# Layer 0 of a two-layer streaming encoder: forgetting attention interleaved with the band attention's projections

## The chip, the cores and the metric

The kernel runs on one core of a Trainium2 chip. The metric is the device time of one execution in microseconds (us), the median of several runs. The engines are named as in the profile: PE (TensorE matmul), PEld (its weight load), DVE (VectorE), ACT (ScalarE), POOL (GpSimd) and SP (SyncE, which issues nearly every DMA here).

## The reference

Two layers of an encoder run over one prompt of 1024 tokens and 8 sample streams of 16 tokens with caches of 512 positions. The change lies in layer 0, cut here to what matters:

```python
def even_proj(h, w_in, b_forget):
    p = h @ w_in                                  # 1152 x 1024 times 1024 x 3080
    qa, ka, va, qb, kb, vb, fa = jnp.split(p, [...], axis=-1)
    logf = jax.nn.log_sigmoid(fa + b_forget)
    ...
# forgetting attention "a": 8 heads of 64, causal, scores + cumsum(logf)[q] - cumsum(logf)[k]
# band attention "b": 8 heads of 64, each chunk of 64 sees itself and 8 chunks to the left, plus a relative bias
y = concat([oa, ob]) @ w_out_even
# sample streams: the 16 new queries of each stream against 512 cached and 16 new keys, in a and in b
```

Then follow a gated feed-forward block, layer 1 with sliding-window attention, another feed-forward block and a final norm.

## The kernel before, in words

Activations lie transposed, channels on the 128 partitions and 1152 tokens along the free dimension. A product at near-float32 precision takes three fp32r matmuls: high part times high part, high times low, low times high (`passes`, lines 166 to 168).

**Projections.** `in_proj` runs "units". A unit 0 to 3 is 128 columns of queries (`proj_q`, line 309), 4 to 7 are 128 columns of keys (`proj_k`, line 344), 8 and 9 are 256 columns of values (`proj_v`, line 361). A q or k unit runs over four chunks of 288 tokens with 24 matmuls each (`chunk_steps`, line 288), a v unit over nine tiles of 128 tokens with 24 matmuls each. Every chunk accumulates in one PSUM bank. `finish` then empties the bank: for keys two ACT copies and a DVE subtraction (lines 348 to 353), for queries an ACT and a DVE instruction (314, 315). The results go to scratch in DRAM by DMA. The bank of a chunk comes from `ps_any`, which goes round the tags m, s, t, s, seven of the eight banks (line 75: s has 3, t 2, m 2, and o has 1).

**Attention.** `prompt_steps` (line 563) yields a head of three steps and then 64 units, each a list of steps: 8 heads of a (the forgetting attention, "fox" below) with four pairs of query tiles, then 8 heads of b. A score step (461) writes 128 queries times up to 1024 keys in banks s and takes the softmax on DVE and ACT. A transpose step (485) turns two key blocks of probabilities and splits them on ACT and DVE, with zeros set by POOL where a block is masked (line 502). A value step (516) multiplies by the values. `attn_load` (427) loads one head.

**Samples.** `sample_steps` (605) handles the 16 pairs of kind and stream. Each loads a cached key tile `skt` and a value tile `svt`. For kind a it also loads a bias tile `sbi`, from which POOL subtracts `cqs` (line 628). A POOL copy spreads the queries into `qbd`.

**Order.** The program states the steps in a written order. `merge` interleaves lists by their weights in proportion. A scheduler of the tile framework then reorders the instructions of each engine by its own model before the program is built. On the chip each engine runs its list strictly in order, and so does SP with its DMA issues. In the kernel before, all units of b's projection are run, then the attention of a and b, with the samples merged along both:

```python
    with sb("pinb", "right") as pin:
        in_proj(1, pin, (0, 1, 8, 2, 3, 9, 4, 5, 6))
        run(pr[0])
        in_proj(1, pin, [7])
    ...
        run(merge(flat(pr[2:]), [(3500, lambda: None)] + sample_steps(pa, qbd, nbs), ...))
```

After layer 0's attention follow the output projection and the feed-forward block (`block_tail`).

Of the kernel before, what the change touches and what calls it, by code (L numbers as in the profile page):

```python
# [11 lines left out]
F32 = mybir.dt.float32  # L12
# [7 lines left out]
P = 128  # L20
D = 1024
KT = D // P
NP = 1024
# [37 lines left out]
def model(ctx: ExitStack, tc: tile.TileContext, I, O):  # L61
# [6 lines left out]
    def sb(name, side="left"):  # L68
        return tc.tile_pool(name=name, bufs=1, side=side, reuse_waits="tile")
# [53 lines left out]
    def nm(s):  # L123
        uid[0] += 1
        return f"{s}_{uid[0]}"
# [32 lines left out]
    def weights(src, shape, other=None, eng=G):  # L158
        f = lambda t: t.rearrange("p (a b) -> p a b", b=shape[1])
        return tuple(f(t) for t in parts(raw_weights(src), other, eng))  # L160
# [123 lines left out]
    def ps_any(tags="msts"):  # L284
        rot[0] += 1
        return ps(tags[rot[0] % len(tags)])
# [19 lines left out]
        return [[((c[3] - c[2]) * 10 // pieces, lambda ci=ci, g=g: part(ci, g)) for g in range(pieces)]  # L306
                for ci, c in enumerate(act)]

    def proj_q(src, act, pool, dst_heads, dst_sample, w=None):
        def finish(o, c0, c1):  # L310
            w = min(c1, NP) - c0
            qh_ = pool.tile([P, c1 - c0], F32R, name=nm("qh"), tag="sth", bufs=2)
            ql_ = pool.tile([P, c1 - c0], F32R, name=nm("ql"), tag="stl", bufs=2)
            A.activation(qh_[:, :w], o[:, :w], AF.Copy, scale=-SCALE)
            V.scalar_tensor_tensor(ql_[:, :w], o[:, :w], -SCALE, qh_[:, :w], ALU.mult, ALU.subtract)
            for r in range(2):
                S.dma_start(dst_heads[r][0:HD, c0:c0 + w], f32(qh_)[r * HD:(r + 1) * HD, :w])
                S.dma_start(dst_heads[r][HD:P, c0:c0 + w], f32(ql_)[r * HD:(r + 1) * HD, :w])
            if c1 > NP:
                qf = pool.tile([P, NS], F32, name=nm("qf"), tag="qf", bufs=1)  # L320
                A.activation(qf, o[:, w:w + NS], AF.Copy, scale=-SCALE)
                S.dma_start(dst_sample, qf)

        return chunk_steps(src, act, ps_any, finish, 1, w)

    def proj_qc(j, act, pool, tiles):

# [13 lines left out]

        return [s_ for l in chunk_steps(I["w_qc"][j], act, lambda: ps("m"), finish, 4) for s_ in l]

    def proj_k(src, act, pool, out, dst_hi, dst_lo, dst_sample, get=ps_any):
        def finish(o, c0, c1):
            w = min(c1, NP) - c0
            kf = pool.tile([P, c1 - c0], F32, name=nm("kf"), tag="kf", bufs=2)
            A.copy(kf, o[:, :c1 - c0])
            S.dma_start(out[:, c0:c1], kf)
            kh_ = pool.tile([P, c1 - c0], F32R, name=nm("khs"), tag="sth", bufs=2)  # L350
            kl_ = pool.tile([P, c1 - c0], F32R, name=nm("kls"), tag="stl", bufs=2)
            A.copy(kh_[:, :w], o[:, :w])
            V.tensor_tensor(kl_[:, :w], o[:, :w], kh_[:, :w], ALU.subtract)
            S.dma_start(dst_hi[:, c0:c0 + w], f32(kh_)[:, :w])
            S.dma_start(dst_lo[:, c0:c0 + w], f32(kl_)[:, :w])
            if c1 > NP:
                S.dma_start(dst_sample, kf[:, w:w + NS])

        return chunk_steps(src, act, get, finish, 1)

    def proj_v(srcs, width, act, pool, nh, dst_out, dst, dst_sample, gate=None):
        per = 4 if len(srcs) == 2 else 8
        ws = [weights(s, (per, width)) for s in srcs]
        wts = [(w[0][:, k, :], w[1][:, k, :]) for w in ws for k in range(per)]
        nv = nh * HD
        for tt in range(T // P):
            t0 = tt * P
            o = ps_any()
            xh_, xl_ = (z[:, :, t0:t0 + P] for z in whole)
            for k in range(KT):  # L370
                E.matmul(o[:, :width], xh_[:, k], wts[k][0], start=k == 0, stop=False)  # L371
                E.matmul(o[:, :width], xh_[:, k], wts[k][1], start=False, stop=False)  # L372
                E.matmul(o[:, :width], xl_[:, k], wts[k][0], start=False, stop=k == KT - 1)  # L373
            vf = pool.tile([P, 256], F32, name=nm("vf"), tag="vf", bufs=2)
            A.copy(vf[:, :nv], o[:, :nv])
            S.dma_start(dst_out[t0:t0 + P], vf[:, :nv])
            if gate is not None:
                V.tensor_tensor(gate[:, tt * 8:(tt + 1) * 8], o[:, 256:264], bfg, ALU.add)
            if tt < NP // P:
                S.dma_start(dst(tt), vf[:, :nv])  # L380
            else:
                S.dma_start(dst_sample, vf[:, :nv])

    def proj_vt(src, act, pool, out, dst_hl, dst_sample):

# [70 lines left out]
        G.tensor_tensor(v[:, :, HD:], vp, v[:, :, :HD], ALU.subtract)  # L456
        return q, kh_, q2, kl2, v, bias

    tiles = [0]

    def score_step(pool, kind, h, tq, un):

        q, kh_, q2, kl2, v, bt = un["hd"]["ins"]
        kb0 = 0 if kind == "a" else max(0, tq - 4)
        n = (tq + 1 - kb0) * P
        tiles[0] += 1
        t = (wp.tile([P, 4 * VW], F32, name=nm("t"), tag="wr", bufs=3) if tiles[0] > 4 and tiles[0] % 3 and (kind == "a" or h < 7 or tq < 4) else
             pool.tile([P, NP], F32, name=nm("t"), tag="t", bufs=4))[:, :NP]
        mins = pool.tile([P, 4], F32, name=nm("mins"), tag="mins", bufs=8)
        segs = []  # L470
        qt = slice(tq * P, (tq + 1) * P)
        for c0, c1 in split(n):
            sp = ps("s")
            w = c1 - c0
            k0 = kb0 * P + c0
            E.matmul(sp[:, :w], q[:, qt], kh_[:, k0:k0 + w], start=True, stop=False)  # L476
            dg = kind == "a" and c1 == n
            E.matmul(sp[:, :w], q2[:, qt], kl2[:, k0:k0 + w], start=False, stop=not dg)  # L478
            if dg:
                E.matmul(sp[:, w - P:w], identb, maskb, start=False, stop=True)  # L480
            segs.append((sp[:, :w], c0, c1, bt[:, 640 - n + c0:640 - n + c1] if bt is not None else
                         zero.to_broadcast([P, w])))
        un[tq] = kb0, t, softmax(pool, t, segs, n, mins)
# [75 lines left out]
    def run(steps):  # L559
        for _, f in steps:  # L560
            f()
# [827 lines left out]
    pq = ExitStack()  # L1389
    pin = pq.enter_context(sb("pina", "right"))  # L1390

    def unit(ki, p, pool, w=None):

        kind = "ab"[ki]
        if p < 4:
            return proj_q(I["w_q"][ki * 4 + p], act, pool, [qs[kind][2 * p], qs[kind][2 * p + 1]],
                          qsm[kind][:, p, :], w)
        p -= 4
        return proj_k(I["w_k"][ki * 4 + p], act, pool, O[f"{kind}_kt"][p * P:(p + 1) * P],
                      kh[kind][p * P:(p + 1) * P], kl[kind][p * P:(p + 1) * P], ksm[kind][:, p, :])  # L1400

    flat = lambda ls: [s_ for l in ls for s_ in l]

    def in_proj(ki, pool, units):
        kind = "ab"[ki]
        for p in units:
            if p < 8:
                run(flat(unit(ki, p, pool)))
                continue
            u = p - 8  # L1410
            first = kind == "a" and u == 0
            src = [I["w_vg"][j] if first else I["w_v"][ki * 2 + u, j] for j in range(2)]
            proj_v(src, VW if first else 256, act, pool, 4, O[f"{kind}_v"][:, u * 256:(u + 1) * 256],
                   lambda tt: vs[kind][:, tt, u * 2:(u + 1) * 2, :],
                   vsm[kind][:, u * 256:(u + 1) * 256], gate if first else None)

    gate = pin.tile([P, 72], F32, name="gate")
    with sb("px0", "right") as px:
# [30 lines left out]
            run(merge(*([flat(f[ci - 1] for f in first)] if ci else []), post[ci], *pre[ci + 1:ci + 2]))  # L1449
        run(flat(f[-1] for f in first))  # L1450
    act = coarse
    in_proj(0, pin, (8, 3, 4, 5, 9))
    forget(nc, pin, nm, ps, gate, ident, ones, I, O, cpd, lsd, csd, cqs)
    in_proj(0, pin, (6, 7))
    pq.close()
    pat = ExitStack()
    pa = pat.enter_context(sb("patin", "right"))
    late = {}
    pr = prompt_steps(pa, late)
    with sb("pinb", "right") as pin:  # L1460
        in_proj(1, pin, (0, 1, 8, 2, 3, 9, 4, 5, 6))
        run(pr[0])
        in_proj(1, pin, [7])
    in0.close()

    xst = ExitStack()
# [2 lines left out]
        xp[h] = xst.enter_context(sb(f"x{h}"))  # L1469
    X = [[None] * 4 for _ in range(2)]  # L1470
    pages, pgs = [], []
    late["p"] = pat.enter_context(sb("patout", "right"))
    with sb("samp", "right") as pa:
        nbs = pa.tile([P, SK], F32, name="nbs")
        S.dma_start(nbs, I["bias_bs"])
        G.tensor_scalar(nbs, nbs, -1.0, 1.0, ALU.mult, ALU.mult)
        qbd = [pa.tile([P, 4, 32], F32, name=f"qbd{i}") for i in range(2)]
        for z in qbd:
            G.memset(z, 0.0)
        run(pr[1])  # L1480
        def behind(f):
            with tc.issue_after(marks["q"].ins):
                f()

        ld = x_load(lambda h, i: I["x"][:, 2 * i:2 * i + 2, h * HALF:(h + 1) * HALF])
        run(merge(flat(pr[2:]), [(3500, lambda: None)] + sample_steps(pa, qbd, nbs), [(4, lambda: None)] + [(1, lambda f=f: behind(f)) for _, f in ld]))
    pat.close()


# [200 lines left out]
```

## Time and profile before

| | us |
|---|---|
| median of 3 runs | 2833.36 (2829.34 to 2841.15) |
| the profiled execution, own time | 2836.8 |
| span of its core, first to last instruction | 2834.7 |
| mean granted TensorE clock, share of 2.4 GHz | 0.977 |
| PE busy | 2712.7 (96%) |
| DVE / ACT / POOL busy | 1697.9 (60%) / 1167.3 (41%) / 1312.6 (46%) |
| projections of b without attention beside them | about 160 to 338 |
| attention of a and b with the samples | about 338 to 700 |

Times of places are counted from the span's start. A PE that is busy all the time is not a PE at its peak, since matmuls are pipelined and their ends are modelled. So the starts of matmuls, their number per us and the weight loads (PEld) are read beside it.

### The profile page before, as it was taken

The numbers are of one execution on the slowest core, as the hardware profiler recorded it, in microseconds if no ns is written. First come the engines' busy times: TensorE is split into PE (matmuls) and PEld (weight loads), VectorE is DVE, ScalarE is ACT, GpSimd is POOL, SyncE is SP. The second block draws the span as 40 slices with busy tenths as digits, with TensorE's granted clock in tenths as the row PEclk, the third lists the DMA queues.
The fourth block names the chain that finished last, engine by engine and source line by source line (L and its number), as shares of the span: only waits on it lengthen the run. The fifth ranks groups of instructions, "written<-read, shape, count | busy, mean of one in ns | idle before, by whom it ended". The sixth has DMA issues, their size and how long they took to land.

```text
span 2834.7 us, 53673 instructions
## 1 busy us (share of the span) xinstructions
PE 2712.7 (96%) x20254; PEld 2563.1 (90%) x20254; DVE 1697.9 (60%) x3676; ACT 1167.3 (41%) x2510; POOL 1312.6 (46%) x1418
## 2 busy tenths in 40 slices
PE   8999999999989999999998999989899999999987
PEld 7999967776989999999998988978799999999987
DVE  7110266666585555656677756663956555566677
ACT  5221367666443222223332467674432222223323
POOL 4212133333444444444998443242444444448993
PEclk8999999999999999999999999999999999999998
DMA  5546579773322222326432232142222232255422
GB/s 158 172 138 199 183 209 261 219 223 106 112 78 72 98 97 95 104 79 232 149 115 80 72 104 62 37 139 62 77 72 100 81 98 100 95 194 182 115 65 93
DMA packets 205971, 349.17 MB, mean 123 GB/s; under 512 B 25992, under 2 KB 136720, under 8 KB 203664
## 3 DMA queue, kind: packets, MB, share of 16 engines
q1 hardware_dynamic: 201104, 341.03, 38.5%
q10 hardware_dynamic: 4608, 4.72, 0.5%
q8 instruction: 159, 2.61, 0.4%
q14 instruction: 100, 0.82, 0.1%
HBM read 243.84 MB, written 101.82 MB: 122 GB/s over the span
## 4 chain that ended last, share of the span: by engine, by line
PE 76%; DVE 9%; POOL 5%; issue 5%; DMA 4%; ACT 2%; SPq 0%; DVEq 0%; POOLq 0%; ACTq 0%
PE ps L166 19%; PE ps L167 19%; PE ps L168 19%; PE ps L499 2%; POOL pg L260 2%; PE ps L478 2%; PE ps L524 1%; PE ps L476 1%; PE ps L372 1%; PE ps L373 1%; PE ps L371 1%; DVE hf L256 1%; PE ps L531 1%; DMA oraw<-od 1%; PE ps L752 1%
## 5 line engine op out<-in xcount | busy, mean ns | idle before, releaser
L166 PE MATMUL ps<-pg,wh 128*128 128x288 f32 x3200 | 951.1, 299 | 42.9 <-DVE x L1257 27.1
L167 PE MATMUL ps<-pg,wh 128*128 128x288 f32 x3200 | 952.2, 298 | 4.0 <-POOL pg L260 2.7
L168 PE MATMUL ps<-pg,wh 128*128 128x288 f32 x3200 | 935.8, 295 | 0.2 <-DVE wh L260 0.2
L166 PEld LDWEIGHTS ps<-pg,wh 128*128 128x128 f32 x3200 | 606.0, 190 | 48.7 <-DVE x L1257 27.6
L167 PEld LDWEIGHTS ps<-pg,wh 128*128 128x128 f32 x3200 | 608.1, 190 | 6.7 <-POOL pg L260 3.5
L168 PEld LDWEIGHTS ps<-pg,wh 128*128 128x128 f32 x3200 | 603.7, 190 | 1.8 <-issue 1.0
L260 POOL TENSOR_TENSOR wh<-wr,wh 128x1024 fp32r<-128x1024 f32 (+1 forms) x96 | 232.9, 2429 | 344.5 <-ACT wh L259 334.5
L259 ACT CAST wh<-wr 128x1024 fp32r<-128x1024 f32 (+2 forms) x156 | 161.3, 1037 | 244.0 <-PE ps L168 218.8
L167 PE MATMUL ps<-hl,wh 128*128 128x288 f32 x832 | 247.4, 299 | 2.5 <-DVE hl L260 2.3
L166 PE MATMUL ps<-hh,wh 128*128 128x288 f32 x832 | 245.7, 301 | 3.4 <-ACT hh L259 3.1
L168 PE MATMUL ps<-hh,wh 128*128 128x288 f32 x832 | 244.9, 296 | 0.0
L260 POOL TENSOR_TENSOR pg<-pg,pg 128x576 fp32r<-128x576 f32 x126 | 193.6, 1551 | 25.6 <-ACT pg L259 24.2
L1257 DVE TENSOR_TENSOR x<-x,ps 128x288 f32<-128x288 f32 x384 | 156.3, 447 | 77.0 <-PE ps L168 76.5
L259 ACT CAST pg<-pg 128x576 fp32r<-128x576 f32 (+1 forms) x134 | 90.6, 701 | 271.2 <-PE ps L168 147.2
L260 POOL TENSOR_TENSOR wh<-x,wh 128x1024 fp32r<-128x1024 f32 x42 | 101.3, 2411 | 150.1 <-ACT wh L259 150.1
L167 PEld LDWEIGHTS ps<-hl,wh 128*128 128x128 f32 x832 | 158.0, 190 | 4.4 <-DVE hl L260 3.4
L166 PEld LDWEIGHTS ps<-hh,wh 128*128 128x128 f32 x832 | 156.5, 190 | 5.5 <-ACT hh L259 5.0
L260 POOL TENSOR_TENSOR x<-wr,x 128x512 fp32r<-128x512 f32 x44 | 58.6, 1331 | 216.5 <-ACT x L259 216.5
L168 PEld LDWEIGHTS ps<-hh,wh 128*128 128x128 f32 x832 | 157.9, 190 | 0.1
L1117 DVE TENSOR_TENSOR u<-p,ps 128x288 f32<-128x288 f32 x176 | 79.0, 449 | 113.3 <-PE ps L168 112.9
L507 DVE TENSOR_TENSOR pl<-ps,ph 128x512 fp32r<-128x512 f32 (+1 forms) x152 | 92.7, 615 | 38.7 <-ACT ph L506 34.2
L166 PE MATMUL ps<-x,wh 128*128 128x288 f32 x352 | 105.7, 300 | 3.8 <-DVE x L1121 3.8
(297 smaller groups left out, 6420.0 us busy)
## 6 DMA issues: line engine op xcount, KB each, us to landing
wr<-w_ffn_in SPq DMA_DIRECT2D x88, 512.0 KB
hds<-hd SPq DMA_DIRECT2D x252, 144.0 KB
pg<-hds SPq DMA_DIRECT2D x126, 288.0 KB
wd<-w_ffn_out SPq DMA_DIRECT2D x36, 512.0 KB
wr<-w_out SPq DMA_DIRECT2D x22, 512.0 KB
xd<-x SPq DMA_DIRECT2D x16, 576.0 KB
x<-xd SPq DMA_DIRECT2D x16, 576.0 KB
svt<-cache_a_v SPq DMA_DIRECT2D x8, 1024.0 KB
```

Of the source, the lines that this page charges most:

```text
L166: E.matmul(out, wh_, xh_, start=first and i == 0, stop=False, skip_group_check=seen)
L167: E.matmul(out, wh_, xl_, start=False, stop=False, skip_group_check=seen)
L168: E.matmul(out, wl_, xh_, start=False, stop=last and i == n - 1, skip_group_check=seen)
L256: V.scalar_tensor_tensor(out, src, gains[:, gi, k:k + 1], rs, ALU.mult, ALU.mult)
L259: A.copy(hi, src)
L260: eng.tensor_tensor(lo, src, hi, ALU.subtract)
L371: E.matmul(o[:, :width], xh_[:, k], wts[k][0], start=k == 0, stop=False)
L478: E.matmul(sp[:, :w], q2[:, qt], kl2[:, k0:k0 + w], start=False, stop=not dg)
L499: E.transpose(pt[:, col:col + P], tl[:, (kb - kb0) * P:(kb - kb0 + 1) * P], ident)
L507: V.tensor_tensor(fl, pt[:, lo_:hi_], fh, ALU.subtract)
L1117: V.tensor_tensor(st[n, q], st["p1", q], st["x", q][:, :QW], ALU.add)
L1257: V.tensor_tensor(z, z, o, ALU.add)
```

## The change

The projections of b become lists of steps like the rest. Units 0 and 1 and the first tile of unit 8 (the first 36 steps) run first, then the head of the attention, and then the other projection steps are merged with attention units 1 to 29 of the list (fox but for its last three units). All projection chunks of b, the first ones too, take their bank from the tag o, of which there is one. The samples are merged with the rest: the last three fox units and the 32 units of b. While projections run, the softmax tiles come from an own tag with five buffers. `proj_v` loads its weights when its first step runs. The cut diff:

```diff
-    def proj_q(src, act, pool, dst_heads, dst_sample, w=None):
+    def proj_q(src, act, pool, dst_heads, dst_sample, w=None, get=None, pieces=1):
...
-        return chunk_steps(src, act, ps_any, finish, 1, w)
+        return chunk_steps(src, act, get or ps_any, finish, pieces, w)
...
-    tiles = [0]
+    tiles, beside = [0], [True]
...
-        t = (wp.tile([P, 4 * VW], F32, name=nm("t"), tag="wr", bufs=3) if tiles[0] > 4 and tiles[0] % 3 and (kind == "a" or h < 7 or tq < 4) else
-             pool.tile([P, NP], F32, name=nm("t"), tag="t", bufs=4))[:, :NP]
+        t = (wp.tile([P, 4 * VW], F32, name=nm("t"), tag="wr", bufs=3) if not beside[0] and tiles[0] % 3 and (h < 7 or tq < 4) else
+             pool.tile([P, NP], F32, name=nm("t"), tag="t", bufs=5))[:, :NP]
...
+    late["p"] = pat.enter_context(sb("patout", "right"))
     pr = prompt_steps(pa, late)
+
+    AHEAD = 30
     with sb("pinb", "right") as pin:
-        in_proj(1, pin, (0, 1, 8, 2, 3, 9, 4, 5, 6))
+        own = lambda: ps("o")
+        proj = in_proj(1, pin, (0, 1, 8, 2, 3, 9, 4, 5, 6, 7), own, 4)
+        head = 36
+        run(proj[:head])
         run(pr[0])
-        in_proj(1, pin, [7])
+        run(merge(flat(pr[1:AHEAD]), proj[head:]))
+    beside[0] = False
     in0.close()
...
-        run(pr[1])
...
-        run(merge(flat(pr[2:]), [(3500, lambda: None)] + sample_steps(pa, qbd, nbs), [(4, lambda: None)] + [(1, lambda f=f: behind(f)) for _, f in ld]))
+        run(merge(flat(pr[AHEAD:]), [(3500, lambda: None)] + sample_steps(pa, qbd, nbs), [(4, lambda: None)] + [(1, lambda f=f: behind(f)) for _, f in ld]))
```

Lines below 306 keep their numbers; line 502 becomes 512, 628 becomes 638, 644 becomes 654.

**PE, from the last projection chunk on.** Before (`hh` and `hl` are the activations, `kh`, `kl` and `q` those of a fox head, `t` a softmax tile):

```order
L166 MATMUL ps_3870<-hh,wh_3765 128x288
L167 MATMUL ps_3870<-hl,wh_3765 128x288
L168 MATMUL ps_3870<-hh,wh_3765 128x288
L476 MATMUL ps_3928<-kh_3712,q_3711 128x384
L478 MATMUL ps_3928<-kl_3713,bt_3720 128x384
L476 MATMUL ps_3931<-kh_3712,q_3711 128x256
L478 MATMUL ps_3931<-kl_3713,bt_3720 128x256
```

and now:

```order
L166 MATMUL ps_5767<-hh,wh_5537 128x288
L167 MATMUL ps_5767<-hl,wh_5537 128x288
L168 MATMUL ps_5767<-hh,wh_5537 128x288
L654 MATMUL ps_6027<-skt_6009,qbd_5856 32x264 x4
L654 MATMUL ps_6045<-skt_6009,qbd_5856 32x264 x4
L486 MATMUL ps_6058<-kh_5861,q_5860 128x384
L488 MATMUL ps_6058<-kl_5862,q_5860 128x384
L665 MATMUL ps_6148<-ident,st_6050 128x128 x4
```

Before, 144 rows of fox steps stand between the last projection matmul and the first score of a sample (line 644). Now that score (line 654), on the key tile `skt` of the first sample, is the next row. The four chunks of the last unit, of which this is the end, now follow each other with no attention row between.

**SP, at the same place.** Before (`ksm_b` is the last store of a projection):

```order
L357 DMA ksm_b<-kf_3895 128x128
L611 DMA qall_4205<-qsm_a 128x512
L611 DMA kall_4207<-ksm_a 128x512
L618 DMA skt_4209<-cache_a_kt 128x4x512
L627 DMA sbi_4215<-csd 128x1x528
```

and now:

```order
L357 DMA ksm_b<-kf_5828 128x128
L899 DMA x_1291_7064<-x 128x2x576
L899 DMA x_1362_7340<-x 128x2x576
L1494 DMA nbs<-bias_bs 128x528
L621 DMA qall_6005<-qsm_a 128x512
L621 DMA kall_6007<-ksm_a 128x512
L628 DMA skt_6009<-cache_a_kt 128x4x512
L637 DMA sbi_6015<-csd 128x1x528
```

The first `skt` still stands behind the stores of the last chunk. Two loads of the residual `x` and the load of `nbs` now stand between them as well.

**PE, at the first projection chunks of b.** Now (each `ps_...` of a projection is the one bank o; of the 24 matmuls of a chunk the end of one and the start of the next stand here):

```order
L167 MATMUL ps_2290<-hl,wh_2188 128x288
L168 MATMUL ps_2290<-hh,wh_2188 128x288
L486 MATMUL ps_2523<-kh_2506,q_2505 128x128
L486 MATMUL ps_2532<-kh_2506,q_2505 128x256
L486 MATMUL ps_2541<-kh_2506,q_2505 128x384
L166 MATMUL ps_2331<-hh,wh_2328 128x288
L167 MATMUL ps_2331<-hl,wh_2328 128x288
```

These are the end of unit 0 and the start of unit 1, with the attention's first three score matmuls between them. The four chunks of unit 0 stand ahead of this with nothing between. From here to the last unit, 9 to some 30 attention rows stand between two chunks.

## Rows read from the trace of the kernel before

**Rows 1.** The page, its part on busy time, for PE.

```profile
PE 2712.7 (96%) x20254; PEld 2563.1 (90%) x20254; DVE 1697.9 (60%) x3676; ACT 1167.3 (41%) x2510; POOL 1312.6 (46%) x1418
```

**Rows 2.** Stretches: length, busy us (xcount) per engine, PE clock, DMA share, GB/s.

```profile
160.00:337.00 177.00, 177.00 (x1393) 176.36 (x1393) 24.43 (x56) 44.20 (x105) 32.67 (x17) 1.00 0.58 176
340.00:420.00 80.00, 74.03 (x563) 56.36 (x563) 51.88 (x172) 51.90 (x117) 31.41 (x89) 0.91 0.78 213
420.00:690.00 270.00, 269.10 (x2155) 194.24 (x2153) 172.67 (x611) 186.98 (x448) 98.53 (x291) 1.00 0.68 205
```

**Rows 3.** Timeline of PE: start, us, instruction, and idle time before with its releaser.

```profile
385.60 0.36 PE L525 MATMUL ps<-pl,v 128*128 128x256 f32 x1
389.76 0.58 PE L524 MATMUL ps<-ph,v 128*128 128x256 f32 x1 [3.80 <-POOL ph L502]
```

**Rows 4.** Timeline of POOL, two starts of line 628.

```profile
351.54 1.07 POOL L628 TENSOR_TENSOR sbi<-sbi,cqs 128x528 f32<-128x528 f32 x1 [4.46 <-DMA sbi<-csd]
...
388.50 1.07 POOL L628 TENSOR_TENSOR sbi<-sbi,cqs 128x528 f32<-128x528 f32 x1 [9.92 <-DMA sbi<-csd]
389.51 0.20 POOL L502 MEMSET ph<- 128x128 f32 x1
```

**Rows 5.** Stretches as in rows 2, of 4 us.

```profile
388.00:392.00 4.00, 2.23 (x7) 1.68 (x8) 0.00 (x0) 0.36 (x1) 3.50 (x10) 0.51 0.10 39
392.00:396.00 4.00, 4.00 (x20) 2.44 (x20) 2.50 (x9) 1.36 (x3) 0.93 (x1) 0.50 0.49 131
```

**Rows 6.** Timeline of PE, last projection matmul and first score of a sample.

```profile
337.63 0.29 PE L168 MATMUL ps<-hh,wh 128*128 128x288 f32 x1
...
361.10 0.65 PE L644 MATMUL ps<-skt,qbd 128*32 128x264 f32 x8
```

**Rows 7.** Timeline of SP's queue behind the last projection chunk.

```profile
339.82 0.45 SPq L357 DMA_DIRECT2D ksm_b<-kf  x1
340.32 0.42 SPq L611 DMA_DIRECT2D qall<-qsm_a  x1
...
341.28 0.62 SPq L618 DMA_DIRECT2D skt<-cache_a_kt  x1
341.94 0.69 SPq L627 DMA_DIRECT2D sbi<-csd  x1
```

**Rows 8.** DMA issues of 320 to 700: all, and sizes of one.

```profile
DMA packets 35848, 76.92 MB, mean 202 GB/s; under 512 B 3225, under 2 KB 13419, under 8 KB 33883
...
skt<-cache_a_kt SPq DMA_DIRECT2D x8, 1024.0 KB
...
x<-x SPq DMA_DIRECT2D x8, 576.0 KB
...
nbs<-bias_bs SPq DMA_DIRECT2D x1, 264.0 KB
qall<-qsm_a SPq DMA_DIRECT2D x1, 256.0 KB
```

**Rows 9.** Stretches as in rows 2, with the DMA full.

```profile
344.00:348.00 4.00, 4.00 (x31) 3.12 (x30) 2.64 (x10) 3.37 (x8) 1.83 (x7) 1.00 0.92 326
348.00:352.00 4.00, 3.40 (x27) 2.99 (x25) 3.04 (x10) 2.96 (x7) 0.46 (x1) 1.00 1.08 224
...
440.00:480.00 40.00, 39.49 (x354) 30.65 (x354) 26.77 (x94) 29.42 (x69) 14.41 (x42) 1.00 0.98 285
```

**Rows 10.** Timelines of PE, ACT and DVE where a key chunk ends.

```profile
334.45 0.29 PE L168 MATMUL ps<-hh,wh 128*128 128x288 f32 x1
334.58 0.29 PE L166 MATMUL ps<-hh,wh 128*128 128x288 f32 x1
...
334.83 0.40 ACT L348 COPY kf<-ps 128x288 f32<-128x288 f32 x1 [2.46 <-PE ps L168]
335.12 0.41 ACT L352 CAST khs<-ps 128x288 fp32r<-128x288 f32 x1
...
335.56 0.46 DVE L353 TENSOR_TENSOR kls<-ps,khs 128x288 fp32r<-128x288 f32 x1 [2.70 <-ACT khs L352]
```

**Rows 11.** Waits of 160 to 337: who waited for whom, us, times, longest.

```profile
ACT qh L314 <- DMA qs_b<-qh: 15.2, 4, 6.4
```

**Rows 12.** The page, its groups: POOL's splits of projection weights.

```profile
L260 POOL TENSOR_TENSOR wh<-wr,wh 128x1024 fp32r<-128x1024 f32 (+1 forms) x96 | 232.9, 2429 | 344.5 <-ACT wh L259 334.5
```

More of the change, by code (lines that the diff above doesn't have):

```diff
@@ L342, in proj_qc, with proj_k @@
         return [s_ for l in chunk_steps(I["w_qc"][j], act, lambda: ps("m"), finish, 4) for s_ in l]
-    def proj_k(src, act, pool, out, dst_hi, dst_lo, dst_sample, get=ps_any):
+    def proj_k(src, act, pool, out, dst_hi, dst_lo, dst_sample, get=ps_any, pieces=1):
         def finish(o, c0, c1):
@@ L357, in finish, with proj_v, part @@
                 S.dma_start(dst_sample, kf[:, w:w + NS])
-        return chunk_steps(src, act, get, finish, 1)
-    def proj_v(srcs, width, act, pool, nh, dst_out, dst, dst_sample, gate=None):
+        return chunk_steps(src, act, get, finish, pieces)
+    def proj_v(srcs, width, pool, nh, dst_out, dst, dst_sample, gate=None, get=None, pieces=1):
         per = 4 if len(srcs) == 2 else 8
-        ws = [weights(s, (per, width)) for s in srcs]
-        wts = [(w[0][:, k, :], w[1][:, k, :]) for w in ws for k in range(per)]
         nv = nh * HD
-        for tt in range(T // P):
+        wts, st = [], {}
+        def part(tt, g):
+            if not wts:
+                ws = [weights(s, (per, width)) for s in srcs]
+                wts.extend((w[0][:, k, :], w[1][:, k, :]) for w in ws for k in range(per))
             t0 = tt * P
-            o = ps_any()
+            if g == 0:
+                st["o"] = (get or ps_any)()
+            o = st["o"]
             xh_, xl_ = (z[:, :, t0:t0 + P] for z in whole)
-            for k in range(KT):
+            for k in range(g * KT // pieces, (g + 1) * KT // pieces):
                 E.matmul(o[:, :width], xh_[:, k], wts[k][0], start=k == 0, stop=False)
@@ L373, in proj_v @@
                 E.matmul(o[:, :width], xl_[:, k], wts[k][0], start=False, stop=k == KT - 1)
+            if g < pieces - 1:
+                return
             vf = pool.tile([P, 256], F32, name=nm("vf"), tag="vf", bufs=2)
@@ L382, in proj_v @@
                 S.dma_start(dst_sample, vf[:, :nv])
+        return [(2860 // pieces, lambda tt=tt, g=g: part(tt, g)) for tt in range(T // P) for g in range(pieces)]
     def proj_vt(src, act, pool, out, dst_hl, dst_sample):
@@ L1390, in model, with unit @@
     pin = pq.enter_context(sb("pina", "right"))
-    def unit(ki, p, pool, w=None):
+    def unit(ki, p, pool, w=None, get=None, pieces=1):
         kind = "ab"[ki]
@@ L1396, in unit, with in_proj @@
             return proj_q(I["w_q"][ki * 4 + p], act, pool, [qs[kind][2 * p], qs[kind][2 * p + 1]],
-                          qsm[kind][:, p, :], w)
+                          qsm[kind][:, p, :], w, get, pieces)
         p -= 4
         return proj_k(I["w_k"][ki * 4 + p], act, pool, O[f"{kind}_kt"][p * P:(p + 1) * P],
-                      kh[kind][p * P:(p + 1) * P], kl[kind][p * P:(p + 1) * P], ksm[kind][:, p, :])
+                      kh[kind][p * P:(p + 1) * P], kl[kind][p * P:(p + 1) * P], ksm[kind][:, p, :],
+                      get or ps_any, pieces)
     flat = lambda ls: [s_ for l in ls for s_ in l]
-    def in_proj(ki, pool, units):
+    def in_proj(ki, pool, units, get=None, pieces=1):
         kind = "ab"[ki]
+        steps = []
         for p in units:
             if p < 8:
-                run(flat(unit(ki, p, pool)))
+                steps += flat(unit(ki, p, pool, None, get, pieces))
                 continue
@@ L1412, in in_proj @@
             src = [I["w_vg"][j] if first else I["w_v"][ki * 2 + u, j] for j in range(2)]
-            proj_v(src, VW if first else 256, act, pool, 4, O[f"{kind}_v"][:, u * 256:(u + 1) * 256],
-                   lambda tt: vs[kind][:, tt, u * 2:(u + 1) * 2, :],
-                   vsm[kind][:, u * 256:(u + 1) * 256], gate if first else None)
+            steps += proj_v(src, VW if first else 256, pool, 4, O[f"{kind}_v"][:, u * 256:(u + 1) * 256],
+                            lambda tt, u=u: vs[kind][:, tt, u * 2:(u + 1) * 2, :],
+                            vsm[kind][:, u * 256:(u + 1) * 256], gate if first else None, get, pieces)
+        return steps
     gate = pin.tile([P, 72], F32, name="gate")
@@ L1451, in model @@
     act = coarse
-    in_proj(0, pin, (8, 3, 4, 5, 9))
+    run(in_proj(0, pin, (8, 3, 4, 5, 9)))
     forget(nc, pin, nm, ps, gate, ident, ones, I, O, cpd, lsd, csd, cqs)
-    in_proj(0, pin, (6, 7))
+    run(in_proj(0, pin, (6, 7)))
     pq.close()
@@ L1471, in model @@
     pages, pgs = [], []
-    late["p"] = pat.enter_context(sb("patout", "right"))
     with sb("samp", "right") as pa:
```

## The prediction

> **What bounds the kernel now.** The page comes first: PE is busy 2712.7 of 2834.7 us [rows 1], so time is won or lost where PE's list is lengthened, shortened or made to wait. Then the stretches of layer 0 [rows 2]. In the projections (160 to 337) PE is busy 177.0 of 177 us with weight loads 176.4. In the attention with samples (420 to 690) it is busy 269.1 of 270. Only the stretch between them is loose: at 340 to 420 PE starts 563 matmuls in 80 us, 7.04 per us, where 420 to 690 has 7.98, and idles 6.0 us. At the steady rate 563 take 70.5 us, so this stretch loses 9.5. Next, what PE waited for there. It stood 3.80 us for a memset of `ph` on POOL [rows 3]. POOL stood 9.92 us for the load of a sample's `sbi`, with that memset queued behind [rows 4]. After the idle time the granted clock was 0.51 and 0.50, the 1.2 GHz level, in 388 to 396, where it had been 1.00 [rows 5]. So the loss is the start of the sample streams: their loads come late, POOL waits in order, PE waits for POOL and then runs at half clock.
>
> The interleaving has little to fill. The Trainium skill ("Perfetto Trace Analysis", Optimization Strategy) advises interleaving where a kernel has regimes whose most-contended engine differs. By busy time the trace shows PE in both regimes, 177.0 of 177 and 269.1 of 270 [rows 2], so the advice does not apply as the rows stand. The case in which it does is the second rival.
>
> **The change, part by part.** No matmul is added or dropped; the sum goes by waits, against the profiled execution's 2836.8 us.
>
> A. *Fox starts without samples.* The 9.5 us leave 340 to 420. If only the idle time went it would be 6.0. Taken: −9.5, as the cause moves away entirely.
>
> B. *The handover.* PE's row behind the last projection matmul is now the first sample's score. Before, that matmul started at 337.63 and the score at 361.10, with 144 fox rows between [rows 6]. Now nothing else can run: PE is in order. The score needs `skt`, which SP issues behind the stores of that last chunk. In the trace the loads began 2.7 us after the matmul (340.32), and `skt` was issued by 341.90 [rows 7]. Now two `x` loads and `nbs` stand ahead, some 1.4 us of issues, so about 5.6 us after the matmul. Ahead of `skt` lie 2 x 576 + 264 + 2 x 256 KB, with it 2952 KB or 3.0 MB [rows 8]. At 326 GB/s that is 9.3 us and at 224 GB/s 13.5 [rows 9], from 2.7 on: landing at 12 to 16 us. The trace bounds it too: `sbi`, issued just behind `skt` at 341.94, let POOL start at 351.54 [rows 4, 7], 10 us after `skt`'s issue, which gives 5.6 + 10 = 16. Ends 10 and 23 (the 23.5 us between the rows 6). Taken: +14.
>
> C. *The sample start in its new place.* `sbi` still lands behind `skt`, POOL still needs 1.07 us for it, and memsets that band steps want stand behind several samples' POOL work. This is the pattern that cost 9.5 us in 340 to 420. After 14 us of idle PE the clock will be at the 1.2 GHz level as in rows 5: 8 us at half clock are 4 us. Ends 4 and 12. Taken: +9.
>
> D. *One bank for all projection chunks.* The next chunk must wait until ACT and DVE have emptied the bank. In a key chunk the last matmul starts at 334.45 and the DVE subtraction ends at 336.02, where the next chunk, in another bank, had started at 334.58 [rows 10]: 1.44 us. Six boundaries have no attention row between (three in unit 0, three in the last unit), two are partly covered: 7 x 1.4 = 10, a little less for queries, which have one ACT instruction fewer: 9. ACT also waited 15.2 us in four pieces for the stores of `qh` to free its two buffers [rows 11]. Before, PE ran on in the other banks; in unit 0 it now waits along. Ends 5 and 20. Taken: +12.
>
> The other 42 or so boundaries (8 units of 4 chunks, 2 of 9 tiles, so 50 in all) I cost at nothing: the attention rows between two chunks cover the 1.4 us. The Trainium skill ("Perfetto Trace Analysis", Matmuls) says that independent groups should rotate through different PSUM banks so that emptying one overlaps the next. The change goes against it; if all 50 were bare they would cost 50 x 1.4 = 70 us by rows 10. That is a rival.
>
> E. *Transfers.* 320 to 700 moved 76.9 MB [rows 8]. About 24 MB of it (fox's loads and stores, projection stores, three `svt` and two band heads loaded ahead, by the sizes in the code) leave, so some 53 MB, the samples' 34 among them, fall beside the band attention. By key-block pairs, 162 of 304 remain there (18 per band head, 18 of the last fox head), 0.53 of 362 us or 192 us, and with both halves of the samples about 215. That asks 247 to 276 GB/s. The trace sustained 285 GB/s at a DMA share of 0.98 with PE losing 0.5 us in 40 [rows 9]. At the 224 GB/s of rows 9 the stage would need 237 us. Ends 0 and +22. Taken: +4, near the row that held 285 for 40 us.
>
> F. *POOL.* Its weight splits of 2.43 us each [rows 12] now stand ahead of fox's memsets, some nine times; a chunk of 24 matmuls (3.2 us) mostly covers one. Ends 0 and 10. Taken: +2.
>
> G. *Fox steps gain cover.* Short waits between its steps shrink. Ends −15 and 0; taken: −3, since 420 to 690 idles 0.9 us [rows 2]. The own tag of softmax tiles and the late loading of value weights change no row of PE's list: 0.
>
> Sum: −9.5 + 14 + 9 + 12 + 4 + 2 − 3 = +28.5: 2865.3 against the profiled 2836.8, and 3.4 less, **2862**, against the median of 2833.4, to which chances and range refer.
>
> **Rivals.** *R1, the samples starve the band stage.* 53 MB do not flow at 250 GB/s between half-partition loads: E is at its upper end and C at 12. For it: 1.08 share at 224 GB/s in rows 9; against it: 285 in the same rows. 2862 + 18 + 3 = 2883, more if POOL's waits repeat.
>
> *R2, faster: hidden weight loads.* The modelled ends flatter PE: the weight loads are busy 194 of 270 us in attention, 72%, but 99.6% in the projections [rows 2]. If the 28% is exposed loading that 24 dense matmuls let the sequencer run ahead of, fox, about 150 of the 362 us, gains up to 42. With B 10, C 4, D 9, E and F 0 and A −9.5 (sum +13.5), 42 gives 2805. It turns the sign from 13.5 us on and passes 0.5% from 28 on. Against it: loads of narrow or 64-column tiles are shorter by themselves, and each attention step keeps its own shapes and waits. The advice on regimes named above would hold in this case.
>
> *R3, nothing measurable.* `skt` lands early (10), the first samples cause no second stall (C 4), banks 5, the rest 0: −9.5 + 19 − 3 = +6.5: 2840.
>
> *R4, every bank boundary bare.* 2862 + 70 − 10 = 2922. Against it: the attention rows between the chunks.
>
> **Numbers.** Chances: forecast 0.56 (2842 to 2878), R1 0.13, R2 0.11, R3 0.15, R4 0.05. A measurement of this kernel tells 0.5% (14 us) from no change: below 2819, above 2848. Slower: forecast nearly whole, R1, R4 and a little of R3, 0.72. Same: 0.18. Faster: 0.10, R2 almost whole. The range leaves out R2, R4 and the tails of R1 and R3: 2836 to 2890. The forecast's own ends are its terms' ends, not all at once: −20 and +16.
>
> **What would show it.** B: one idle stretch of PE of 10 to 16 us right behind the last matmul of line 168 on `hh`, released by the load of `skt`, then a granted clock of 0.5. If PE idles under 5 us there, B is wrong. C: POOL's line 638 released by `sbi`, and PE waiting for line 512 within 30 us after. D: gaps of 1 to 1.5 us between chunks of unit 0 and of the last unit, released by DVE; gaps at the middle chunks would mean R4. A: 7.9 matmuls per us or more from the first fox step on. E: a DMA share above 0.9 through the band stage with PE waiting for loads would mean R1. G and R2: PEld's share where fox and projections mix, above 90% for R2. A total below 2836 would mean that a gain of fox's steps beat the handover.

## The result, and the profile after

The change takes 2857.38 us (median of 4 runs, 2855.11 to 2863.96) where the kernel before took 2831.35 (4 runs). The ratio is 1.0086, with a 95% interval of 1.0069 to 1.0104: slower by some 24 us by the ratio, 26 by these two medians. The forecast was 2862, in 2836 to 2890.

The profiled executions (2855.1 and 2836.8 us) differ by 18.3 us, their spans by 18.6. All of it stands before the output projection: its first matmul started at 703.10 us before, and starts at 721.85 now. The page of the changed kernel, its part on busy time for PE, answers to [rows 1]:

```profile
PE 2717.8 (95%) x20254; PEld 2566.5 (90%) x20254; DVE 1700.1 (60%) x3676; ACT 1168.1 (41%) x2510; POOL 1309.3 (46%) x1418
```

PE's work is the same. The stretches of the changed kernel (length, busy us and count of PE, PEld, DVE, ACT, POOL, then granted clock, DMA share, GB/s) show where it stands still, against [rows 2, 5]:

```profile
200.00:440.00 240.00, 238.81 (x1815) 219.83 (x1815) 118.33 (x368) 130.47 (x283) 72.14 (x142) 1.00 0.50 140
...
484.00:488.00 4.00, 0.11 (x1) 0.00 (x0) 0.32 (x1) 0.59 (x2) 0.35 (x2) 1.00 0.63 193
488.00:492.00 4.00, 0.00 (x0) 0.00 (x0) 0.00 (x0) 0.00 (x0) 0.00 (x0) 0.52 1.02 370
...
500.00:504.00 4.00, 2.76 (x18) 0.97 (x10) 1.42 (x6) 0.81 (x3) 1.86 (x5) 0.50 0.90 277
504.00:508.00 4.00, 3.93 (x24) 2.16 (x24) 0.73 (x4) 1.35 (x5) 1.42 (x3) 0.50 0.95 263
...
560.00:700.00 140.00, 139.83 (x1188) 94.58 (x1188) 81.07 (x294) 90.28 (x226) 50.78 (x156) 1.00 0.76 252
```

Projections and fox together (200 to 440) keep PE busy 99.5% of the time, and the band attention with the samples (560 to 700) 99.9%. Between them lies a hole of 15 us, and in it and behind it the granted clock is at 0.50 to 0.52, the 1.2 GHz level (called half clock from here on). PE's waits of 160 to 700, all of them (who waited for whom, us in total, times, longest; `st` is the softmax tile of a sample, `kls`, `ql` and `qf` are what empties a projection's bank):

```profile
PE ps L654 <- DMA skt<-cache_a_kt: 15.4, 1, 15.4
PE ps L166 <- DVE kls L353: 4.0, 3, 1.3
PE ps L166 <- DVE ql L315: 3.0, 3, 1.0
PE ps L665 <- ACT st L429: 1.3, 1, 1.3
PE ps L166 <- ACT qf L321: 1.1, 1, 1.1
```

The timeline of SP around the hole (start, us, instruction), against [rows 7]:

```profile
484.14 0.33 SPq L646 DMA_DIRECT2D svt<-cache_a_v  x1
...
487.02 1.05 SPq L899 DMA_DIRECT2D x<-x  x2
488.11 0.54 SPq L1494 DMA_DIRECT2D nbs<-bias_bs  x1
489.78 0.34 SPq L621 DMA_DIRECT2D qall<-qsm_a  x1
490.92 0.33 SPq L621 DMA_DIRECT2D kall<-ksm_a  x1
491.29 0.60 SPq L628 DMA_DIRECT2D skt<-cache_a_kt  x1
491.94 0.68 SPq L637 DMA_DIRECT2D sbi<-csd  x1
```

The last projection matmul started at 483.81, the issue of the first `skt` ended at 491.89, and the score on it started at 499.54, 15.7 us after that matmul. The last row of this kind is POOL's first subtraction from `sbi`, against [rows 4]:

```profile
500.89 1.07 POOL L638 TENSOR_TENSOR sbi<-sbi,cqs 128x528 f32<-128x528 f32 x1 [4.09 <-DMA sbi<-csd]
```

### The profile page after: what moved, and what is told of

It reads as the page before. It is cut to its first block, busy times and chain, and to the rows that moved or that the text cites. A ratio compares the mean times of both kernels' runs of the same rounds, so it can differ in the third digit from the quotient of the medians.

```text
span 2853.3 us, 53592 instructions
## 1 busy us (share of the span) xinstructions
PE 2717.8 (95%) x20254; PEld 2566.5 (90%) x20254; DVE 1700.1 (60%) x3676; ACT 1168.1 (41%) x2510; POOL 1309.3 (46%) x1418
## 4 chain that ended last, share of the span: by engine, by line
PE 61%; DVE 7%; POOL 6%; issue 4%; DMA 4%; ACT 1%; SPq 0%; DVEq 0%; POOLq 0%; ACTq 0%
PE ps L166 16%; PE ps L167 16%; PE ps L168 16%; POOL pg L260 2%; POOL wh L260 1%; PE ps L509 1%; PE ps L762 1%; PE ps L488 1%; PE ps L679 1%; PE ps L534 1%; DVE h L256 1%; PE ps L744 1%; PE ps L486 1%; DMA oraw<-od 1%; DMA pg<-hds 1%
## 5 line engine op out<-in xcount | busy, mean ns | idle before, releaser
L166 PE MATMUL ps<-hh,wh 128*128 128x288 f32 x832 | 247.5, 303 | 11.4 <-DVE kls L353 4.0
L166 PEld LDWEIGHTS ps<-hh,wh 128*128 128x128 f32 x832 | 156.7, 190 | 15.7 <-ACT hh L259 5.0
```

Of the source, the lines that this page charges most:

```text
L166: E.matmul(out, wh_, xh_, start=first and i == 0, stop=False, skip_group_check=seen)
```

## The experiments

Each starts from the changed kernel. "Before" in the ratios is the kernel before, run beside it on the same chip.

| run | median us | ratio to before, 95% interval |
|---|---|---|
| xlate | 2856.93 | 1.0080, 1.0063 to 1.0097 |
| banks0 | 2847.83 | 1.0047, 1.0029 to 1.0065 |
| banks7 | 2853.07 | 1.0066, 1.0048 to 1.0084 |
| apart | 2826.02 | 0.9979, 0.9961 to 0.9996 |
| warm | 2857.19 | 1.0077, 1.0062 to 1.0091 |
| banksall | 2837.38 | 1.0016, 1.0005 to 1.0028 |
| mix16 | 2830.25 | 0.9985, 0.9975 to 0.9996 |
| xlate_warm | 2858.20 | 1.0084, 1.0062 to 1.0107 |
| apart38 | 2839.90 | 1.0021, 1.0009 to 1.0033 |
| apart22 | 2829.39 | 0.9988, 0.9975 to 1.0001 |
| sbifirst | 2858.67 | 1.0093, 1.0073 to 1.0114 |
| sbifirst_warm | 2857.25 | 1.0089, 1.0070 to 1.0108 |

**apart: the samples' new place without the interleaving.**

```diff
-        own = lambda: ps("o")
+        own = ps_any
-        run(proj[:head])
+        run(proj)
         run(pr[0])
-        run(merge(flat(pr[1:AHEAD]), proj[head:]))
     beside[0] = False
     in0.close()
+    run(flat(pr[1:AHEAD]))
```

> All projections of b first, in all banks, as in the kernel before; then the first 29 attention units with nothing beside them; then the rest with the samples, as in the change. Theory (PE bounds every part, so the interleaving itself gives nothing and the loss is the handover and the one bank): no stall of 15 us and no bank gaps; the start of the samples costs some 5 us; fox alone keeps PE busy over 98%: 2828 to 2838, the kernel before within 0.3%. Rival (fox needs other work beside it to cover its softmax): PE idles in fox by itself, 10 us or more in short waits for DVE and ACT, and the time is 2845 or more; then the interleaving is worth what apart loses.

It took 2826.02 us, 0.2% less than before and some 31 us less than the change, just below the range of the theory. PE's timeline and waits of 160 to 700:

```profile
473.15 1.10 PE L654 MATMUL ps<-skt,qbd 128*32 128x264 f32 x16
...
692.98 0.61 PE L166 MATMUL ps<-pg,wh 128*128 128x288 f32 x1 [5.23 <-ACT wh L259]
```

```profile
PE ps L166 <- ACT wh L259: 5.2, 1, 5.2
PE ps L509 <- DVE pl L517: 2.3, 9, 0.3
PE ps L509 <- ACT t L429: 0.9, 1, 0.9
```

Its two stretches with fox alone:

```profile
338.00:420.00 82.00, 80.03 (x570) 66.32 (x571) 67.45 (x221) 63.82 (x143) 31.52 (x87) 1.00 0.63 167
420.00:473.00 53.00, 51.96 (x368) 42.86 (x366) 42.62 (x138) 40.12 (x90) 20.29 (x55) 1.00 0.51 128
```

The first score waits for nothing. Fox by itself leaves PE idle for 3 us in these 135, not 10. So the new place of the samples is a gain, and the interleaving as it is written turns it into a loss: from the same matmul shortly ahead of b's projections (the 1037th, at 157.4 to 157.9 us) to the first of the output projection the kernel before took 545.2 us, apart 535.6, the change 564.0. The profiled execution of apart (2821.6) is one of the fastest of its twelve; by the ratio its gain over the kernel before is 6 us, by the interval 1 to 11. Apart keeps the other edits of the change (the softmax tiles' own tag while projections run, the later loads of value weights); no run takes them out.

**mix16: interleaving that ends early.** The banks are those of banksall (below); only fox units 1 to 15 are merged with projections.

```diff
-        run(merge(flat(pr[1:AHEAD]), proj[head:]))
+        run(merge(flat(pr[1:16]), proj[head:]))
     beside[0] = False
     in0.close()
+    run(flat(pr[16:AHEAD]))
```

> The projections are interleaved with the first 15 fox units only, in the banks of banksall; 14 fox units then run alone, and the samples start where the change starts them. Theory: the loads of the samples have 50 us of fox to hide behind, so there is no stall and no half clock, and of the 3.7 us that the interleaving gains half or all is kept against apart (2826): 2822 to 2826. Rival (with twice the projection work per attention unit the chunks follow each other bare, or the value steps wait for banks m): waits of 5 to 10 us in all between 190 and 420, 2831 to 2836.

It took 2830.25, 4 us above the range of the theory, and by the intervals not to be told from apart. In the profile the stretch from a matmul of unit 0 to the first score of a sample, with equally many matmuls between in both kernels, took 275.4 us (195.30 to 470.65) against 278.4 in apart (194.72 to 473.15). The interleaving gives 3 us there. They do not last: from that score to the first matmul of the output projection mix16 takes 223.0 us and apart 219.8, so that both stand at 535.6 us for the whole stretch.

```profile
693.64 0.61 PE L166 MATMUL ps<-pg,wh 128*128 128x288 f32 x1 [5.29 <-ACT wh L259]
```

The two part only in the last 55 us of it, where their orders differ and mix16 has a mean clock of 0.95 (640 to 693.6), apart 0.98. No run shows the 3 us in a time. The rival's waits did not show: those of PE before the output projection are 2 us in all.

**banks0 and banks7: more banks at one end.** In banks0 units 0 and 1 take theirs from all tags; in banks7 the last unit goes round o and m.

```diff
-        proj = in_proj(1, pin, (0, 1, 8, 2, 3, 9, 4, 5, 6, 7), own, 4)
+        proj = in_proj(1, pin, (0, 1), ps_any, 4) + in_proj(1, pin, (8, 2, 3, 9, 4, 5, 6, 7), own, 4)
```

> Units 0 and 1 take their banks from all tags again, the others stay in the one bank. Theory (the one bank makes PE wait between chunks that follow each other): the four gaps of 0.99 to 1.10 us at 188 to 202 are gone and nothing takes their place, 4 us less, about 2853; the handover stays at 15 us. Rival (the two buffers of qh and their stores hold the chunks anyway): the gaps come back behind ACT or a store, and the time stays at 2857.

```diff
-        proj = in_proj(1, pin, (0, 1, 8, 2, 3, 9, 4, 5, 6, 7), own, 4)
+        proj = in_proj(1, pin, (0, 1, 8, 2, 3, 9, 4, 5, 6), own, 4) + in_proj(1, pin, [7], lambda: ps_any("om"), 4)
```

> The chunks of the last unit go round the tags o and m, three banks. By the written program some 80 attention rows now stand on PE between the last projection matmul and the first score of a sample. Theory (one bank made the order that leaves the handover bare): three gaps of 1.33 us are gone (4 us), 80 rows at 0.125 us cover 10 of the 15.4 us, so some 5 us of stall are left, and with the shorter stall some 3 us of half clock go: 17 us less, about 2840. Rival (those rows are missing where they stood before, ahead of the chunks): new gaps between the last chunks or waits for banks m in the value steps take it back, 2852 to 2857.

banks0 took 2847.83, 10 us less than the change where 4 were expected. Its waits of PE of 160 to 700:

```profile
PE ps L654 <- DMA skt<-cache_a_kt: 15.8, 1, 15.8
PE ps L488 <- DMA kl<-cpd: 1.8, 1, 1.8
```

The gaps of both ends are gone, not only the first; the 10 us are near what seven boundaries cost, 8 us of idle time. (The profiled execution, 2852.3, is the slowest of seven, and up to the output projection it is only 1.7 us ahead of the change.) The attention starts 18 us later (its first score at 219.1 us, 200.6 in the change), so that more of it is left for the last chunks. The handover stayed, at 15.8 us, as expected.

banks7 took 2853.07, 4 us less where 17 were expected. The same view:

```profile
PE ps L654 <- DMA skt<-cache_a_kt: 5.9, 1, 5.9
PE ps L166 <- DVE kls L353: 4.5, 5, 1.3
```

The handover shrank to 5.9 us as computed, and the rival held as well: five gaps of up to 1.33 us appeared at chunks still in the one bank, where the rows stood that now cover the handover. The profiled execution (2844.9) is the fastest of six; the others take 2852.7 to 2855.7, so what the shorter stall is worth in the usual execution this run does not settle.

**banksall: more banks everywhere.**

```diff
-        proj = in_proj(1, pin, (0, 1, 8, 2, 3, 9, 4, 5, 6, 7), own, 4)
+        proj = in_proj(1, pin, (0, 1), ps_any, 4) + in_proj(1, pin, (8, 2, 3, 9, 4, 5, 6, 7), lambda: ps_any("om"), 4)
```

> Units 0 and 1 take banks from all tags, all others from o and m. By the written program 103 attention rows stand between the last projection matmul and the first score of a sample. Theory (one bank and a bare handover are the whole loss): the gaps of unit 0 (3.8 us) and of the last unit (4 us) are gone, 103 rows cover 12.9 of the 15.4 us, some 3 us of stall and up to 5 us lost at half clock are left. Against apart that is -3.7 for the interleaving, +3 and +5: 2830, in 2824 to 2838. Rival (as in banks7, what covers the handover is missing ahead of it, or value steps now wait for banks m): new gaps of 5 us or more in all between 190 and 470, 2843 or more.

2837.38, in the expected range: more banks (two more for eight units, those of all tags for the first two), with nothing else touched, give 20 us back. PE's timeline at the first score, and the stretch behind it:

```profile
478.44 1.32 PE L654 MATMUL ps<-skt,qbd 128*32 128x264 f32 x16 [2.23 <-DMA skt<-cache_a_kt]
```

```profile
480.00:506.00 26.00, 25.75 (x125) 15.75 (x125) 9.48 (x37) 9.34 (x24) 9.10 (x23) 0.50 0.88 258
```

The stall is 2.23 us. The profiled execution, the slowest of 12 (2848.1), was then at half clock for 26 us; the median execution has a mean granted clock of 0.976 to 0.977 where this one has 0.972.

**xlate: fewer bytes ahead of the first sample.**

```diff
-            [(4, lambda: None)] + [(1, lambda f=f: behind(f)) for _, f in ld]))
+            [(12, lambda: None)] + [(1, lambda f=f: behind(f)) for _, f in ld]))
```

> Only the two loads of x that stood ahead of the first sample's loads on SP start later. Theory (the handover lasts as long as the transfers ahead of the first skt): the stall of PE behind the last projection matmul, 15.4 us, shrinks by their two issues (1.1 us) and by 1152 KB at the 370 to 406 GB/s of that stretch (2.9 to 3.2 us), to about 11.3 us, and the kernel by 4 us to about 2853. Rival (skt waits for memory to come free, or for the stores): the stall stays within 1 us of 15.4 and the time at 2857.

The stall shrank to 11.43 us, as worked out in sum (`skt` was issued 1.8 us sooner and was there 2.2 us sooner after its issue). No gain shows in the time, 2856.93; six runs tell some 5 us, so that a gain of 4 is not excluded. PE's timeline, and the stretches behind:

```profile
495.01 1.99 PE L654 MATMUL ps<-skt,qbd 128*32 128x264 f32 x16 [11.43 <-DMA skt<-cache_a_kt]
500.36 1.11 PE L665 MATMUL ps<-ident,st 128*128 128x128 f32 x4 [2.12 <-ACT st L429]
```

```profile
495.00:500.00 5.00, 3.23 (x18) 1.24 (x18) 1.42 (x6) 0.52 (x1) 1.86 (x5) 0.50 1.01 282
500.00:508.00 8.00, 7.64 (x46) 4.01 (x46) 2.77 (x11) 3.66 (x11) 2.21 (x6) 0.50 0.85 238
508.00:516.00 8.00, 8.00 (x41) 4.76 (x41) 2.39 (x8) 2.35 (x5) 2.82 (x8) 0.51 0.65 227
516.00:540.00 24.00, 24.00 (x213) 16.07 (x212) 13.96 (x53) 15.51 (x40) 7.76 (x24) 1.00 0.67 211
```

PE worked 21 us at half clock behind the shorter stall, where it worked some 9 in the profile of the change. At half speed the 12 us more are worth some 6 (an estimate from these rows), as much as the shorter stall gave or more. Whether the other executions of xlate did the same is not shown.

**warm and xlate_warm: the stall filled with matmuls of no use.**

```diff
         run(merge(flat(pr[1:AHEAD]), proj[head:]))
+        warm = ps("o")
+        for _ in range(240):
+            E.matmul(warm[:, :P], identb, maskb, start=True, stop=True)
```

> 240 small bf16 matmuls of no use stand on PE between the last projection matmul and the first score of a sample; nothing else moves. Theory (the stall costs twice, first as idle time and then as half clock): they fill the stall, the granted clock stays at 1.00 behind it, and the 9.2 us that PE then worked at half clock (499.5 to 508.7) shrink to 4.6: about 2852. In the median more, if other executions of the change stayed at half clock as long as xlate (20.9 us of work) or banks0 (19.4): 2847 to 2852. Rival (the clock falls for another reason than the stall, or the loads keep the stretch slow): 0.5 still stands behind the stall and the time stays at 2857.

> The two edits of xlate and warm together: the two loads of x start later, and 200 small matmuls of no use fill the stall. Theory (behind the stall two things pace PE, the loads and POOL work of the first samples, and the half clock, and each hides the other: warm took away only the second, xlate only the first): now both are gone, the fourth turn of a sample that ends the first 60 us comes 4 us sooner than in the change, and the time is 2852 to 2854. Rival (the sample start is paced by something that neither touches): 2857 as in both alone.

(xlate_warm has 200 of them, and xlate's edit.) Both stayed where the change is: 2857.19 and 2858.20, so the theory that the two causes hide each other was not borne out; in the profile of xlate_warm PE waited 3.33 us for `st`, and half clock followed for 17 us. PE's timeline of warm:

```profile
483.72 13.56 PE L1485 MATMUL ps<-maskb,identb 128*128 128x128 bf16 x240 [1.08 <-DVE kls L353]
499.13 1.10 PE L654 MATMUL ps<-skt,qbd 128*32 128x264 f32 x16 [1.85 <-DMA skt<-cache_a_kt]
...
504.18 1.11 PE L665 MATMUL ps<-ident,st 128*128 128x128 f32 x4 [3.21 <-ACT st L429]
```

The clock stayed at 1.00 to 501, so the first scores took 1.10 us in place of 1.99. PE then waited 3.21 us for the softmax of that sample in place of 1.31, and in that wait the clock fell. The first sample was through (line 687, the transpose of its output, called its turn) 33.4 us after the last projection matmul, 32.0 in the change. In warm half clock lasted 6.8 us in all, in the change 20.5.

The Trainium skill ("TensorE: Matmul & The Clock Gate", Terms) counts what the clock costs as the time at the lower level times the part of the pulses lost. By that, as an estimate, the 13.7 us less would be worth 6.8. The runs here do not show it, 2857.19 against 2857.38: for 11.3 us of the 20.5 (488.2 to 499.5) PE had nothing to run in the change, and what the faster scores gained in warm went into longer waits for `skt` (it came 16.8 us after the last projection matmul, 15.7 in the change) and for `st`.

**sbifirst and sbifirst_warm: the bias tile first.**

```diff
         def load(kind, b, un):
+            if kind == "a":
+                un["bias"] = bias = pool.tile([P, SK], F32, name=nm("sbi"), tag="sbi", bufs=2)
+                src = csd[b * 8:(b + 1) * 8, :]
+                S.dma_start(bias, bass.AP(src.tensor, src.offset, [[SK, 8], [0, 16], [1, SK]]))
+                G.tensor_tensor(bias, bias, cqs[:, b:b + 1].to_broadcast([P, SK]), ALU.subtract)
...
             S.dma_start(kt[:, :, :PAST], I[f"cache_{kind}_kt"][b])
```

> The bias tile sbi of a sample is loaded, and subtracted from by POOL, ahead of its skt instead of behind it; nothing else moves. Theory (the first samples are paced by sbi: in the change it reaches POOL at 500.9, 506.5 and 511.2, 1.4 us or more after the score that needs it): the first two sbi are ready when the scores are, the wait of PE for st (1.3 us) goes, the first turn of a sample, 32.0 us behind the last projection matmul, comes 2 to 5 us sooner, and the time is 2852 to 2855. Rival (the half clock paces the stretch): the first turn stays within 1 us of 32.0 and the time at 2857.

> sbifirst and the 240 matmuls of warm together. Theory (sbi and the half clock each hide the other): PE neither waits for st nor falls to half clock behind the stall, the first turn of a sample comes 5 to 8 us sooner than 32.0, and the time is 2849 to 2853. Rival (the loads of skt and svt pace the first samples whatever sbi and the clock do): the first turn comes at 31 to 33 us, with PE waiting for skt of the second or third sample, and the time stays at 2857.

PE's timeline of sbifirst_warm:

```profile
502.24 1.99 PE L653 MATMUL ps<-skt,qbd 128*32 128x264 f32 x16 [3.67 <-DMA skt<-cache_a_kt]
...
505.84 1.11 PE L664 MATMUL ps<-ident,st 128*128 128x128 f32 x4 [0.38 <-ACT st L429]
```

The wait for `st` went, 3.21 to 0.38, and `skt` came 1.8 us later than in warm: the first turn stands at 33.3 us, with warm's 33.4. The time is 2857.25. In sbifirst, without the filling, the profiled execution was at half clock from 485.5 to 526.5 and its first turn came at 38.8 us; the median is 2858.67. So neither the clock nor the order of its two loads brings the first sample nearer to the last projection matmul: 32.0 us in the change, 33.3 to 38.8 in warm and these two, 34.8 and 35.6 in xlate and xlate_warm. That points to the transfers as a whole (a DMA share of 0.94 or more from that matmul to the first score in all of them), of which these runs moved no more than 1152 KB; it is not shown. What the bare handover by itself costs in time, apart from the banks, stays open as well: no run removes it alone.

**apart38 and apart22: the samples denser and less dense.** From apart; in apart22 the number is 22.

```diff
-    AHEAD = 30
+    AHEAD = 38
```

> As apart, but the samples lie beside the last 26 band units alone (38 instead of 30 units ahead of them). By the bytes that is some 50 MB in 190 us, 263 GB/s, where the trace of the kernel before held 285 for 40 us. Theory (the transfers of the samples have room beside the band attention, so term E is near 0): within 5 us of apart, 2821 to 2832. Rival (the samples starve PE when they are packed): loads of skt and svt hold PE in many places, 2838 or more.

> As apart, but the samples start 8 units sooner, beside the last 11 fox units too. Theory (it was the start in the first fox heads, with the loads of the head and the last stores, that cost the kernel before its 10 us; once it starts later, the place does not matter): 2823 to 2830, as apart. Rival (beside fox the samples hold POOL, whose memsets fox needs): the stall of PE for a memset comes back at the new place, 4 us or more with the half clock behind it, 2832 or more.

apart22 took 2829.39, within its range, and PE waits for no memset: beside fox the samples can lie as well, if they do not start in its first heads. apart38 took 2839.90, above the range; the stretches where it loses:

```profile
560.00:600.00 40.00, 40.00 (x362) 27.71 (x361) 20.80 (x79) 25.37 (x66) 15.12 (x48) 1.00 1.00 318
600.00:640.00 40.00, 37.62 (x300) 24.47 (x298) 18.44 (x63) 19.64 (x52) 10.77 (x36) 0.79 0.99 312
```

At 318 GB/s and a DMA share of 1.00 PE still loses nothing; in the next 40 us, at 312 GB/s, it idles 2.4 us and loses clock. Its waits there are for the splits of probabilities on ACT, each under 1 us, and not for loads, so the rival's price held and its mechanism was not seen; that the traffic is the cause is not shown.

## Why the prediction was right

The sum said +28.5 us; the ratio of the result says +24. By the profiles, the stretch to the output projection grew by 18.8: −9.6 from before to apart, and +28.5 from apart to the change. The terms behind A were to add up to 38. By the profiles they are 28.5 and by the medians 31, and A by the ratio is 6 and not 9.5. So the forecast has its sign and its two main prices (B and D) from the right mechanism; that its sum came within 5 us is in part luck, since the terms that were too high and A stand against each other.

**A, right that it is a gain; its size was worked out in a wrong way.** apart takes away the sample start in the first fox heads: −9.6 in the profiles, −6 by the ratio, −9.5 said. But the 9.5 came from a steady rate of 7.98 matmuls per us, which is that of fox, band and samples mixed. Fox alone has 6.9 in apart (938 in 135 us) with PE busy 98%, less than the 7.04 of the stretch that was to be slow. So the fit to 9.6 is luck; what [rows 2] show there is 6.0 us of idle time and a clock of 0.91. The mark that was given for A, 7.9 matmuls per us, fails for the same reason: 200 to 440 has 7.56, while PE idles 1.2 us in 240.

**B, right in size, in part for other reasons.** 15.4 us idle, 15.7 from start to start, where 14 was said, released by `skt` as said, with the clock at 0.52 and 0.50 after it. But `skt` was issued 8.1 us after the last matmul, not 5.6: the issues of `qall` and `kall` waited 1.1 us for a `svt` of 1024 KB and 0.8 us for a store. That `svt`, issued at 484.14, was missing from the sum of bytes. From its issue on `skt` took 7.6 us, where the 14 left 8.4. xlate shows that the length of the stall follows the loads ahead of `skt`, their issues and their bytes.

**C, right that it costs, wrong in how.** POOL's line 638 waited for `sbi` as said, but no memset held PE. The softmax of the first sample did, 1.3 us, and PE worked 9 us at half clock. What apart and the change leave for C, E, F and G together, behind the handover (15.6) and the bank waits (9.2), is some 4 us, where 9 + 4 + 2 − 3 = 12 was said. No run tells C from the others. Taking away most of the half clock (warm) or the wait for `sbi` (sbifirst_warm) brought no time back.

**D, right at the boundaries, too high in sum.** Seven boundaries wait, 0.99 to 1.10 us of idle time at queries and 1.33 at keys. From start to start the key boundaries take 1.62 us, 1.49 more than the 0.13 between two matmuls elsewhere, where 1.44 was said: 9.2 us more in all seven, 9 said. The further 3 us for ACT waiting on the stores of `qh` did not come. No middle chunk waits: R4 is out. banksall (20 us) shows that the one bank costs more than its gaps. With three banks for the last unit (banks7) 89 attention rows stand at the handover, where the change has none, and gaps open at the chunks that had them: the one bank makes the order hand attention rows to the earlier chunks. That link was not in the prediction.

**E and F, too high.** With the samples beside the band attention, PE is busy 139.83 of 140 us at 252 GB/s, so E is near 0, the lower end. Of POOL's weight splits no wait is seen. R1's price came only at apart38's density, and not by waits for loads.

**G, right in size within the mix, not shown in the time**: −3 said, −3 by mix16 up to the first sample, nothing by the output projection. R2 is out: no hidden gain of tens of us. Its mark failed too: PEld's share is 91.6% in 200 to 440, above the 90% given. But projections with 99.6% are half of that stretch, and fox alone has 81% (apart, 338 to 473), which makes 90% without any gain. The Trainium skill ("Perfetto Trace Analysis", Optimization Strategy), weighed in the prediction, advises interleaving for regimes bound by different engines; here both were PE's, and those 3 us are what it gave. The other rule of the Trainium skill weighed there ("Perfetto Trace Analysis", Matmuls), to rotate groups through banks, is borne out: in banks0 the four waits of units 0 and 1 (4.1 us) are gone. In banksall's 20 us the rows at the handover have their part.

## What to carry to other kernels

Before two stages are interleaved, look at the end of the mix: what work is left to cover the loads of the stage that follows? Here a single buffer for one of the two streams not only made it wait; it let the other stream run ahead and left the tail bare. And where the engine that bounds both stages is the same, expect little: the better half of this change was to move the samples away from the start of the attention, which alone is 0.2% faster than the kernel before and has the lowest median of the versions run.

## What was not expected of the hardware

How long the granted clock stayed at 0.5 did not follow the length of the stall before it. After 15.4 us without work it was down for 20.5 us in all (488.2 to 508.7), after 11.4 us for 27.3 (xlate), after 2.2 us for 27.3 (banksall), and after 17.1 us for 41.0 (sbifirst). In the last three PE was at work for 20 us and longer, busy nine tenths of it or more by its modelled ends, before the clock rose. The spread of one kernel goes with it: banksall's executions run from 2834.2 us at a mean clock of 0.979 to 2848.1 at 0.972.
